# Experts' activations: 32 by 32 block transposes on VectorE in place of TensorE transposes, with the down weights' rows in the matching order

## The chip, the core and the metric

The kernel runs on one core of a Trainium2 chip. The metric is the device time of one execution in microseconds, lower is better. Before the change three timed runs gave 1387.32, 1388.30 and 1388.99 us, a median of 1388.3. All numbers are 32-bit floating point (some products use a split into a high and a low part).

## The reference

The model is a two-layer trunk on 256 tokens of width 1024. Layer 0 has an attention mixer and a dense feed-forward part, layer 1 a state-space mixer and a mixture of eight experts, of which each token takes its best two. The change lies in the experts:

```python
def moe_swiglu(h, w_router, w_gate, w_up, w_down):
    logits = (h @ w_router).astype(jnp.float32)
    top_val, top_idx = lax.top_k(logits, TOP_K)
    weights = jax.nn.softmax(top_val, axis=-1)
    gates = jnp.sum(jax.nn.one_hot(top_idx, N_EXPERTS, dtype=jnp.float32) * weights[..., None], axis=-2)
    out = jnp.zeros_like(h)
    for e in range(N_EXPERTS):
        out = out + gates[..., e:e + 1] * swiglu(h, w_gate[e], w_up[e], w_down[e])
    return out
```

Here `swiglu(h, g, u, d)` is `(silu(h @ g) * (h @ u)) @ d`. Gate and up weights are 1024 x 2816 for each expert, down weights 2816 x 1024.

## The kernel before

The experts are ranked by how many tokens chose them, and each rank has room for a fixed number of groups of 32 tokens: 4, 3, 3, 3, 3, 2, 2, 2 (`CAPS`). "Expert 0" below is the first rank. An expert's 2816 hidden columns are worked off in three blocks (`b`): 1024, 1024 and 768 (512 + 256).

For each block TensorE first does the gate and up products (`gate_up`, L1676). The tokens of group i are the stationary operand, 128 x 32, and the weights move. A weight unit is 128 rows by 1024 columns, 512 KB, one DMA. Its columns are cut in four pieces, each of which goes to its own 32 columns of the array, and so to its own 32 partitions of the result. So the PSUM bank `gu[i]` holds, at partition 32j + t, token t's columns of the j-th quarter. In the profile each such product is two records. ScalarE and VectorE then make silu(gate) * up of it (L1703 to L1708) in the tile `eh`, still with 32 tokens in each quarter of the partitions.

The down product (`down`, L1723) needs the hidden columns on the partitions, so `eh` is transposed between (`trans`, L1710): TensorE transposes 128 x 128 pieces into PSUM (L1715, L1717, and L1719 for the 64-row piece of the third block), and ScalarE or VectorE copy them to `hT` (L1721). `eh` and `hT` are two halves of one tile and both bear the name `eh` in the profile. There is one copy of each.

The order is written out in `experts` (L1742 to L1757): gate and up of block b, the down product of the block before, the transposes of block b, and so on. The transposes of block b thus stand between a down product and the next gate product, and their result is first read a whole gate and up product later. Only the very last down product (L1771) follows its transposes directly.

Other work, such as gathering the next expert's tokens (L1591), selecting them (L1580), multiplying the down result by its gate (L1627) and scattering it back (L1649), is put into a queue with a count of weight units and is issued between units (`run_queue`).

Weights come through one list of transfers on the SP queue in the order of use (L171). A transfer is issued when a buffer is free: 4 + 15 buffers, and two pairs (`hT_hi`, `hT_lo`) that earlier stages lend, 23 of 512 KB in all. A buffer is given back when TensorE has read it (`release`). After the experts stands a branch (`overflow`, L1788) for tokens that found no room; it was not taken in the profiled execution.

Of the kernel before, what the change touches and what calls it, by code (L numbers as in the profile page):

```python
# [12 lines left out]
AF = mybir.ActivationFunctionType  # L13
OP = mybir.AluOpType
AX = mybir.AxisListType

D = 1024
# [3 lines left out]
NE = 8  # L21
# [11 lines left out]
CAPS = (4, 3, 3, 3, 3, 2, 2, 2)  # L33
# [40 lines left out]
S_SW, S_W2, S_FB, S_B2, S_GN, N_SMALL = 0, 192, 448, 449, 451, 579  # L74


def layout(inputs):

    r = {n: np.ascontiguousarray(inputs[n]) for n in _INS}
    col = lambda v: v.reshape(-1, 128).T  # L80
    c = make_consts()
    c[:, C_C:C_C + 8] = col(inputs["c"])
    r["consts"] = c
    r["vecs"] = np.concatenate([inputs[m.replace("mod", "norm")].reshape(-1, 128) for m in NORMS]
                               + [inputs[m + "_b"].reshape(-1, 128) for m in NORMS])
    s = np.zeros((128, N_SMALL), np.float32)
    w = inputs["e_w_in"][0]
    s[:, S_SW:S_SW + 192] = np.concatenate([w[:, 1536:1544], w[:, 3080:3096]], axis=1).reshape(8, 128, 24) \
        .transpose(1, 0, 2).reshape(128, 192)
    s[40:56, S_W2:S_W2 + 256] = inputs["e_gla_w2"][0]  # L90
    for i in range(4):
        s[32 * i:32 * i + 8, S_FB] = inputs["e_fox_fb"].reshape(8)
    s[:, S_B2:S_B2 + 2] = col(inputs["e_gla_b2"])
    s[:, S_GN:S_GN + 128] = inputs["e_gla_norm"].reshape(1, 128)
    r["smalls"] = s

    st = lambda z: z.reshape(32, 2, 64).transpose(1, 2, 0).reshape(128, 32)
    dt = np.broadcast_to(inputs["o_log_dt"].reshape(32, 2, 1), (32, 2, 64))
    d = np.zeros((128, 32), np.float32)
    d[96:128] = inputs["o_d_skip"].reshape(32, 32).T  # L100
    r["s5par"] = np.concatenate([st(inputs["o_lam_re"]), st(inputs["o_lam_im"]), st(dt), d], axis=1)
    b = [inputs[n].reshape(32, 2, 64, 16).transpose(1, 2, 0, 3).reshape(128, 512) for n in ("o_b_re", "o_b_im")]
    c = [inputs[n].reshape(32, 2, 16, 64).transpose(1, 3, 0, 2).reshape(128, 512) for n in ("o_c_re", "o_c_im")]
    r["s5bc"] = np.concatenate(b + c, axis=1)


    z = np.stack([inputs["o_exp_gate"][0], inputs["o_exp_up"][0]], axis=2).reshape(NE, NCH, 128, 2, FF)
    z5 = z[..., 2 * D:2 * D + 512].reshape(NE, NCH, 128, D)
    z2 = z[..., 2 * D + 512:].reshape(NE, 4, 2, 128, 512).transpose(0, 1, 3, 2, 4).reshape(NE, 4, 128, D)
    r["o_exp_rest"] = np.concatenate([z5, z2], axis=1)  # L110
    return r


# [129 lines left out]
class Trunk:  # L243
# [1412 lines left out]
    def experts(self):  # L1656


        nc, ex, st, mm = self.nc, self.ex, self.st, self.nc.tensor.matmul
        do = lambda n, fn, *args: self.queue.append([n, lambda: fn(*args)])  # L1660
        hid = ex.tile([128, 2, 4, 256], F32, name="eh", tag="z", bufs=2)
        eh, hT = hid[:, 0], hid[:, 1]
        cg = lambda j: slice(32 * j, 32 * j + 32)
        bank = lambda n: self.psum.tile([128, 512], F32, name=n, tag=n, bufs=1)
        gu, dn = [bank(f"gu{i}") for i in range(4)], [bank(f"dn{i}") for i in range(2)]
# [10 lines left out]
        def gate_up(e, b):  # L1676
            xT = self.xT[e]
            def wide(o):
                def emit(i, k, raw):
                    for j in range(4):  # L1680
                        mm(gu[i][cg(j), o:o + 256], xT[:, k, cg(i)], raw[:, 256 * j:256 * j + 256],  # L1681
                           start=(o == 0 and k == 0), stop=(o > 0 and k == NCH - 1))
                return emit

            def rest(i, u, raw):
                for h in range(2):
                    for j in range(4):
                        w = raw[:, 512 * h + 128 * j:512 * h + 128 * j + 128]
                        if u < 8:
                            mm(gu[i][cg(j), 128 * h:128 * h + 128], xT[:, u, cg(i)], w, start=(u == h == 0),  # L1690
                               stop=False)
                        else:
                            mm(gu[i][cg(j), 256:384], xT[:, 2 * u - 16 + h, cg(i)], w, start=False,
                               stop=(u == 11 and h == 1))

            if b < 2:
                for n, o in (("o_exp_gate", 0), ("o_exp_up", 256)):
                    group(e, [(n, e, b, k) for k in range(NCH)], wide(o))
            else:
                group(e, [("rest", e, b, k) for k in range(12)], rest)  # L1700
            for i in range(CAPS[e]):
                w = 256 if b < 2 else 128
                nc.scalar.activation(eh[:, i, 0:w], gu[i][:, 0:w], AF.Silu)  # L1703
                nc.vector.tensor_tensor(out=eh[:, i, 0:w], in0=gu[i][:, w:2 * w], in1=eh[:, i, 0:w], op=OP.mult)  # L1704
                if b == 2:
                    o = eh[64:128, i, 128:256]
                    nc.scalar.activation(o, gu[i][0:64, 256:384], AF.Silu)
                    nc.vector.tensor_tensor(out=o, in0=gu[i][64:128, 256:384], in1=o, op=OP.mult)  # L1708

        def trans(e, b):  # L1710
            for x in range(0, CAPS[e], 2):
                n = min(2, CAPS[e] - x)
                p = self.ps([128, 2, 256])
                for i in range(n):
                    nc.tensor.transpose(p[:, i, 0:128], eh[:, x + i, 0:128], self.ident)  # L1715
                    if b < 2:
                        nc.tensor.transpose(p[:, i, 128:256], eh[:, x + i, 128:256], self.ident)  # L1717
                    else:
                        nc.tensor.transpose(p[:, i, 128:192], eh[64:128, x + i, 128:256], self.ident[64:128, 64:128])  # L1719
                w = 256 if b < 2 else 192  # L1720
                (nc.vector.tensor_copy if x else nc.scalar.copy)(hT[:, x:x + n, 0:w], p[:, :n, 0:w])  # L1721

        def down(e, b):  # L1723
            n = 8 if b < 2 else 6
            def emit(i, f, raw):
                c = (128 * (f % 2) + 32 * (f // 2)) if b < 2 else 32 * f
                for j in range(4):
                    mm(dn[i // 2][cg(j), 256 * (i % 2):256 * (i % 2) + 256], hT[:, i, c:c + 32],  # L1728
                       raw[:, 256 * j:256 * j + 256], start=(b == f == i % 2 == 0),
                       stop=(b == 2 and f == n - 1 and (i % 2 == 1 or i == CAPS[e] - 1)))  # L1730

            group(e, [("down", e, b, f) for f in range(n)], emit)
# [48 lines left out]
    def overflow(self):  # L1781

        nc, kp, ex, I = self.nc, self.keep, self.ex, self.ins
# [4 lines left out]
        with self.tc.If(self.most > 0):  # L1788
            for first in (0.0, 128.0):
                v.memset(cur, 1.0)  # L1790
                with self.tc.For_i(0, NE, 1) as e:
# [18 lines left out]
                    for k in range(NCH):  # L1810
                        p = self.ps()
# [4 lines left out]
                    p = self.ps()  # L1816
# [2 lines left out]
                        nc.tensor.transpose(p[:, 128 * t:128 * t + 128], P[:, t, :], self.ident)  # L1819
                    v.tensor_copy(B.rearrange("p t j -> p (t j)"), p[:, 0:256])  # L1820
                    dn = self.dn
                    raw = lambda n: self.rawpool.tile([128, D], F32, name=n, tag="raw", bufs=4)
                    w3 = lambda n, f: (I[n][0, bass.ds(e, 1), :, 128 * f:128 * f + 128]
                                       .rearrange("o (k p) f -> p (o k) f", p=128))
                    for f in range(FF // 128):
                        wg, wu, wd = raw("og"), raw("ou"), raw("od")
                        gv, uv = (z.rearrange("p (k f) -> p k f", k=NCH) for z in (wg, wu))
                        nc.sync.dma_start(out=gv, in_=w3("o_exp_gate", f))
                        nc.sync.dma_start(out=uv, in_=w3("o_exp_up", f))
                        nc.sync.dma_start(out=wd, in_=I["o_exp_down"][0, bass.ds(e, 1), 128 * f:128 * f + 128, :]  # L1830
                                          .rearrange("o p d -> p (o d)"))
                        b = self.ps()
                        for i, z in enumerate((gv, uv)):
                            for k in range(NCH):
                                nc.tensor.matmul(b[:, 128 * i:128 * i + 128], z[:, k, :], xT[:, k, :], start=(k == 0),
                                                 stop=(k == NCH - 1))
                        h = kp.tile([128, 2, 128], F32, name="oh2", tag="t2k", bufs=4)
                        a.activation(h[:, 0, :], b[:, 0:128], AF.Silu)
                        v.tensor_tensor(out=h[:, 1, :], in0=h[:, 0, :], in1=b[:, 128:256], op=OP.mult)
                        for x in range(2):  # L1840
                            nc.tensor.matmul(dn[x], h[:, 1, :], wd[:, 512 * x:512 * x + 512], start=(f == 0),
                                             stop=(f == FF // 128 - 1))
# [4 lines left out]
                    for t in range(2):  # L1847
                        for x in range(2):
                            hs = slice(512 * x, 512 * x + 512)
                            p = self.ps()  # L1850
# [346 lines left out]
```

## Time and profile before

| | |
|---|---|
| timed runs, median (range) | 1388.3 us (1387.32 to 1388.99) |
| profiled execution | 1385.76 us, of which the span of the program is 1384.0 us |
| TensorE products | 1254.3 us busy, 91% of the span |
| VectorE | 599.9 us, 43% |
| ScalarE | 380.6 us, 28% |
| bytes moved by DMA | 398.59 MB, mean 288 GB/s |
| mean granted TensorE clock | 0.956 of 2.4 GHz |

The experts' part runs from about 640 us to the end. A busy time says how long an engine had at least one instruction under way; the busy shares of the whole span mix this part with the earlier stages, in which VectorE has far more to do, so the parts are looked at one by one. Times in the rows below are counted from the span's start. "PE" is TensorE's product stream, "PEld" its loads of the stationary operand, DVE VectorE, ACT ScalarE, SPq the queue of the engine that issues the weights' transfers.

### The profile page before, as it was taken

The page shows a single profiled execution, that of the slowest core. Times are in us where ns is not written, and L with a number is a line of the kernel's source. Part 1 is how long each engine was busy: PE and PEld are TensorE (multiplying, and loading weights), DVE is VectorE, ACT ScalarE, POOL GpSimd, SP SyncE. Part 2 cuts the span into 40 slices and gives each one's busy share as a digit, 9 for nine tenths or more (in the row PEclk, how much of TensorE's full clock was granted, in tenths as well). Part 3 has the DMA queues.
Part 4 walks back from the last instruction along what each step waited for, and adds up shares of the span by engine and source line. Part 5 has one row for each costly group of instructions (what it writes and reads, how often), then busy time and mean ns, then how long its engine had stood idle before and what let it go on. Part 6 is the DMA issues. An engine that isn't in the chain of part 4 may idle for free. (4 is left out here: it accounts for less than half of the span.)

```text
span 1384.0 us, 42896 instructions
## 1 busy us (share of the span) xinstructions
PE 1254.3 (91%) x18767; PEld 956.9 (69%) x18767; DVE 599.9 (43%) x1023; ACT 380.6 (28%) x832; POOL 267.3 (19%) x324
## 2 busy tenths in 40 slices
PE   5998988789896878889989999999999999999985
PEld 4976777678795778775676676575586586756552
DVE  6998798678889685651000210210200202111113
ACT  4455444455543566520010110110010011101001
POOL 1000036999859252000000000000000000000000
PEclk9998999899998888999999999999999999999998
DMA  9866648678785211339998989989989989999994
GB/s 346 278 224 228 198 135 262 208 249 268 251 276 180 92 62 48 107 116 407 407 385 311 366 311 352 399 298 372 392 295 391 375 310 401 407 406 407 407 407 186
DMA packets 138723, 398.59 MB, mean 288 GB/s; under 512 B 12288, under 2 KB 45312, under 8 KB 138400
## 3 DMA queue, kind: packets, MB, share of 16 engines
q1 hardware_dynamic: 138176, 394.62, 78.7%
q8 instruction: 149, 2.44, 0.7%
q0 software_dynamic: 208, 1.15, 0.3%
q14 instruction: 46, 0.38, 0.1%
q10 hardware_dynamic: 144, 0.00, 0.0%
HBM read 394.67 MB, written 1.05 MB: 286 GB/s over the span
## 5 line engine op out<-in xcount | busy, mean ns | idle before, releaser
L1704 DVE TENSOR_TENSOR eh<-gu,eh 128x256 f32<-128x256 f32 (+1 forms) x66 | 25.1, 380 | 433.5 <-ACT eh L1703 432.9
L280 PE MATMUL ps<-hT_hi,hl 128*128 128x256 f32 x576 | 172.0, 299 | 16.1 <-ACT hT_hi L839 7.6
L205 DVE TENSOR_TENSOR hl<-raw,hl 128x1024 fp32r<-128x1024 f32 x121 | 158.5, 1316 | 61.1 <-ACT hl L198 59.3
L281 PE MATMUL ps<-hT_lo,hl 128*128 128x256 f32 x576 | 169.2, 294 | 3.0 <-DVE hT_lo L840 2.5
L282 PE MATMUL ps<-hT_hi,hl 128*128 128x256 f32 x576 | 168.8, 293 | 3.2 <-DVE hl L205 3.1
L1681 PE MATMUL gu<-raw,xTs 128*32 128x256 f32 x3032 | 168.7, 380 | 1.5 <-DMA raw<-in_o_exp_up_dram 1.5
L385 POOL TENSOR_TENSOR ss<-ss 128x1 f32<-128x1 f32 x10 | 2.7, 275 | 862.3 <-ACT ps L378 779.2
L198 ACT ACTIVATE hl<-raw 128x1024 fp32r<-128x1024 f32 x121 | 126.9, 1058 | 144.2 <-PE ps L282 32.3
L1681 PEld LDWEIGHTS gu<-raw,xTs 128*32 128x32 f32 x3032 | 97.3, 110 | 67.4 <-DMA raw<-in_o_exp_up_dram 3.9
L280 PEld LDWEIGHTS ps<-hT_hi,hl 128*128 128x128 f32 x576 | 115.7, 201 | 19.5 <-ACT hT_hi L839 8.1
L1728 PE MATMUL dn<-raw,eh 128*32 128x256 f32 x2032 | 119.1, 380 | 3.1 <-issue 2.0
L281 PEld LDWEIGHTS ps<-hT_lo,hl 128*128 128x128 f32 x576 | 115.6, 201 | 5.0 <-DVE hT_lo L840 3.4
L282 PEld LDWEIGHTS ps<-hT_hi,hl 128*128 128x128 f32 x576 | 115.3, 200 | 4.6 <-DVE hl L205 4.5
L1728 PEld LDWEIGHTS dn<-raw,eh 128*32 128x32 f32 x2032 | 69.7, 110 | 46.2 <-issue 6.6
L1703 ACT ACTIVATE eh<-gu 128x256 f32<-128x256 f32 (+1 forms) x66 | 23.0, 348 | 267.6 <-PE gu L1681 237.5
L1721 ACT COPY eh<-ps 128x512 f32<-128x512 f32 (+1 forms) x24 | 13.2, 550 | 231.7 <-PE ps L1717 155.0
L1681 PE MATMUL gu<-rawh,xTs 128*32 128x256 f32 x992 | 56.1, 380 | 0.6 <-DMA rawh<-in_o_exp_up_dram 0.6
L1721 DVE COPY eh<-ps 128x256 f32<-128x256 f32 (+3 forms) x15 | 6.8, 451 | 108.0 <-PE ps L1717 54.1
L1690 PE MATMUL gu<-raw,xTs 128*32 128x128 f32 x1664 | 51.5, 278 | 1.3 <-DMA raw<-in_o_exp_rest_dram 0.8
L1627 DVE TENSOR_TENSOR y<-dn,gate 32x256 f32<-32x256 f32 x88 | 36.9, 419 | 31.9 <-PE dn L1728 30.6
L1690 PEld LDWEIGHTS gu<-raw,xTs 128*32 128x32 f32 x1664 | 45.7, 112 | 4.7 <-DMA raw<-in_o_exp_rest_dram 2.3
L1681 PE MATMUL gu<-rawi,xTs 128*32 128x256 f32 x848 | 47.5, 379 | 0.0
(425 smaller groups left out, 2222.0 us busy)
## 6 DMA issues: line engine op xcount, KB each, us to landing
raw<-in_o_exp_down_dram SPq DMA_DIRECT2D x92, 512.0 KB, 8.9
raw<-in_o_exp_gate_dram SPq DMA_DIRECT2D x68, 512.0 KB, 6.2
raw<-in_o_exp_up_dram SPq DMA_DIRECT2D x67, 512.0 KB, 6.3
raw<-in_o_exp_rest_dram SPq DMA_DIRECT2D x58, 512.0 KB, 10.1
rawi<-in_o_exp_down_dram SPq DMA_DIRECT2D x30, 512.0 KB, 5.9
rawh<-in_o_exp_down_dram SPq DMA_DIRECT2D x27, 512.0 KB, 6.2
raw<-in_e_mod_ffn_w_dram SPq DMA_DIRECT2D x24, 512.0 KB, 4.4
raw<-in_o_mod_mix_w_dram SPq DMA_DIRECT2D x24, 512.0 KB, 4.6
```

Source lines behind the costliest of these rows:

```text
L198: nc.scalar.activation(hi, raw, AF.Copy)
L205: nc.vector.tensor_tensor(out=lo, in0=raw, in1=hi.bitcast(F32), op=OP.subtract)
L280: mm(out, lh, rh, start=start, stop=False)
L281: mm(out, lh, rl, start=False, stop=False)
L282: mm(out, ll, rh, start=False, stop=stop)
L1627: self.nc.vector.tensor_tensor(out=self.y[32 * i:32 * i + 32, cs], in0=self.dn[i // 2][js, o:o + 256], in1=self.gate[js, cs], op=OP.mult)
L1681: mm(gu[i][cg(j), o:o + 256], xT[:, k, cg(i)], raw[:, 256 * j:256 * j + 256], start=(o == 0 and k == 0), stop=(o > 0 and k == NCH - 1))
L1690: mm(gu[i][cg(j), 128 * h:128 * h + 128], xT[:, u, cg(i)], w, start=(u == h == 0), stop=False)
L1703: nc.scalar.activation(eh[:, i, 0:w], gu[i][:, 0:w], AF.Silu)
L1704: nc.vector.tensor_tensor(out=eh[:, i, 0:w], in0=gu[i][:, w:2 * w], in1=eh[:, i, 0:w], op=OP.mult)
L1721: (nc.vector.tensor_copy if x else nc.scalar.copy)(hT[:, x:x + n, 0:w], p[:, :n, 0:w])
L1728: mm(dn[i // 2][cg(j), 256 * (i % 2):256 * (i % 2) + 256], hT[:, i, c:c + 32], raw[:, 256 * j:256 * j + 256], start=(b == f == i % 2 == 0) ...
```

## The change

`trans` becomes one VectorE transpose for each group of tokens. It turns every 32 x 32 block of the tile in its place and moves no block to other partitions. With w columns in a quarter, the block at partitions 32j.. and columns 32f.. then holds hidden columns j*w + 32f + r on its rows r, so one slice of 32 columns of `hT` has, on its 128 partitions, four runs of 32 hidden columns that lie w apart. The host lays the rows of the down weights out in this order (`down_order`), so each transfer of 128 rows stays as it was. In the third block the last 256 columns are four quarters of 64 with gate and up side by side, so that its short operations are 128 x 64 and not 64 x 128. In the overflow branch one transfer becomes four.

```diff
+def down_order():
+    return np.concatenate([r0 + np.arange(4 * w).reshape(4, w // 32, 32).transpose(1, 0, 2).reshape(-1)
+                           for r0, w in ((0, 256), (D, 256), (2 * D, 128), (2 * D + 512, 64))])
...
-    z2 = z[..., 2 * D + 512:].reshape(NE, 4, 2, 128, 512).transpose(0, 1, 3, 2, 4).reshape(NE, 4, 128, D)
+    z2 = z[..., 2 * D + 512:].reshape(NE, 4, 2, 128, 2, 4, 64).transpose(0, 1, 3, 2, 5, 4, 6).reshape(NE, 4, 128, D)
...
+    r["o_exp_down"] = np.ascontiguousarray(r["o_exp_down"][:, :, down_order()])
...
-                    o = eh[64:128, i, 128:256]
-                    nc.scalar.activation(o, gu[i][0:64, 256:384], AF.Silu)
-                    nc.vector.tensor_tensor(out=o, in0=gu[i][64:128, 256:384], in1=o, op=OP.mult)
+                    o = eh[:, i, 128:192]
+                    nc.scalar.activation(o, gu[i][:, 256:320], AF.Silu)
+                    nc.vector.tensor_tensor(out=o, in0=gu[i][:, 320:384], in1=o, op=OP.mult)
...
         def trans(e, b):
-            for x in range(0, CAPS[e], 2):
-                n = min(2, CAPS[e] - x)
-                p = self.ps([128, 2, 256])
-                for i in range(n):
-                    nc.tensor.transpose(p[:, i, 0:128], eh[:, x + i, 0:128], self.ident)
-                    if b < 2:
-                        nc.tensor.transpose(p[:, i, 128:256], eh[:, x + i, 128:256], self.ident)
-                    else:
-                        nc.tensor.transpose(p[:, i, 128:192], eh[64:128, x + i, 128:256], self.ident[64:128, 64:128])
-                w = 256 if b < 2 else 192
-                (nc.vector.tensor_copy if x else nc.scalar.copy)(hT[:, x:x + n, 0:w], p[:, :n, 0:w])
+            w = 256 if b < 2 else 192
+            for i in range(CAPS[e]):
+                nc.vector.transpose(hT[:, i, 0:w], eh[:, i, 0:w])
...
-                c = (128 * (f % 2) + 32 * (f // 2)) if b < 2 else 32 * f
+                c = 32 * f
...
-                        nc.sync.dma_start(out=wd, in_=I["o_exp_down"][0, bass.ds(e, 1), 128 * f:128 * f + 128, :]
-                                          .rearrange("o p d -> p (o d)"))
+                        for i in range(4):
+                            r0 = rows.index(128 * f + 32 * i)
+                            nc.sync.dma_start(out=wd[32 * i:32 * i + 32], in_=I["o_exp_down"][0, bass.ds(e, 1),
+                                              r0:r0 + 32, :].rearrange("o p d -> p (o d)"))
```

TensorE's instructions of the kernel before, at the end of the down product that follows expert 4's first gate and up block (`dn` is the down result, `ps` the transposes' bank, `cst` holds the identity, `gu` the gate and up result):

```order
L1728 MATMUL dn_6284<-rawh,eh 32x256 x8
L1728 MATMUL dn_6285<-rawh,eh 32x256 x4
L1715 MATMUL ps_11556<-cst,eh 128x128
L1717 MATMUL ps_11556<-cst,eh 128x128
L1715 MATMUL ps_11556<-cst,eh 128x128
L1717 MATMUL ps_11556<-cst,eh 128x128
L1715 MATMUL ps_11562<-cst,eh 128x128
L1717 MATMUL ps_11562<-cst,eh 128x128
L1681 MATMUL gu_6280<-rawh,xTs 32x256 x4
L1681 MATMUL gu_6281<-rawh,xTs 32x256 x4
```

The same place on TensorE in the changed kernel, whose lines are numbered anew (the down product is L1729, the gate and up product L1689):

```order
L1729 MATMUL dn_6284<-rawh,eh 32x256 x8
L1729 MATMUL dn_6285<-rawh,eh 32x256 x4
L1689 MATMUL gu_6280<-rawh,xTs 32x256 x4
L1689 MATMUL gu_6281<-rawh,xTs 32x256 x4
L1689 MATMUL gu_6282<-rawh,xTs 32x256 x4
```

The six transposes are gone, and the gate product follows the down product directly.

VectorE's instructions of the kernel before, one section later in expert 4 (`X` is the result that the scatter is added to, `P` the next expert's selection):

```order
L1654 TENSOR_TENSOR X<-ps_11889,X 128x512
L1654 TENSOR_TENSOR X<-ps_11920,X 128x512
L1721 COPY eh<-ps_11943 128x256
L1580 TENSOR_SCALAR P<-cst,rpp 128x128 x2
L1704 TENSOR_TENSOR eh<-gu_6280,eh 128x128
L1708 TENSOR_TENSOR eh<-gu_6280,eh 64x128
```

The same place on VectorE in the changed kernel:

```order
L1662 TENSOR_TENSOR X<-ps_11795,X 128x512
L1662 TENSOR_TENSOR X<-ps_11826,X 128x512
L1722 STREAM_TRANSPOSE eh<-eh 128x256 x3
L1588 TENSOR_SCALAR P<-cst,rpp 128x128 x2
L1712 TENSOR_TENSOR eh<-gu_6280,eh 128x128
```

One copy out of PSUM has become three transposes from `eh` to `hT`, ahead of the selection for the next expert.

TensorE's instructions of the kernel before around the last transposes, those of expert 7's third block:

```order
L1728 MATMUL dn_6284<-hT_lo,eh 32x256 x16
L1715 MATMUL ps_14862<-cst,eh 128x128
L1719 MATMUL ps_14862<-cst,eh 128x64
L1715 MATMUL ps_14862<-cst,eh 128x128
L1719 MATMUL ps_14862<-cst,eh 128x64
L1728 MATMUL dn_6284<-raw_14432,eh 32x256 x8
```

The same place on TensorE in the changed kernel:

```order
L1729 MATMUL dn_6284<-hT_hi,eh 32x256 x16
L1729 MATMUL dn_6284<-hT_lo,eh 32x256 x16
L1729 MATMUL dn_6284<-raw_14296,eh 32x256 x8
L1729 MATMUL dn_6284<-raw_14306,eh 32x256 x8
L1729 MATMUL dn_6284<-raw_14316,eh 32x256 x8
```

Here the last down product stands directly behind the one before it, with VectorE's two transposes of 128 x 192 between them in time.

## Rows read from the trace of the kernel before

**Rows 1.** Windows: us, busy us of PE, PEld, DVE, ACT, POOL; clock; DMA share; GB/s.

```profile
700.00:720.00 20.00, 15.60 (x381) 14.75 (x377) 0.00 (x0) 1.67 (x6) 0.00 (x0) 0.83 1.02 406
...
860.00:880.00 20.00, 20.00 (x366) 12.01 (x360) 6.59 (x16) 2.46 (x5) 0.00 (x0) 1.00 1.03 405
...
1100.00:1120.00 20.00, 20.00 (x475) 16.55 (x478) 2.20 (x5) 3.16 (x9) 0.00 (x0) 1.00 0.81 284
...
1160.00:1180.00 20.00, 20.00 (x344) 11.35 (x340) 8.07 (x17) 2.80 (x5) 0.00 (x0) 1.00 1.03 407
```

**Rows 2.** Waits of the DMA queue, 640 to 1384 us: us in total, times, longest.

```profile
SPq L171 <- PE gu L1681: 112.1, 159, 2.4
```

**Rows 3.** Waits of PE, 640 to 1384 us.

```profile
PE gu L1693 <- issue: 8.2, 8, 1.7
...
PE gu L1681 <- DMA raw<-in_o_exp_up_dram: 1.5, 5, 0.7
```

**Rows 4.** Timeline of PE, expert 4, first block: start us, us, engine, line, operation.

```profile
1063.40 6.66 PE L1728 MATMUL dn<-rawh,eh 128*32 128x256 f32 x120
1069.99 0.33 PE L1715 MATMUL ps<-cst,eh 128*128 128x128 f32 x1
...
1070.59 0.27 PE L1717 MATMUL ps<-cst,eh 128*128 128x128 f32 x1
1070.79 1.50 PE L1681 MATMUL gu<-rawh,xTs 128*32 128x256 f32 x24
```

**Rows 5.** Timeline of PE around four other sections of transposes.

```profile
641.70 3.64 PE L1681 MATMUL gu<-hT_hi,xTs 128*32 128x256 f32 x64
...
646.67 3.66 PE L1681 MATMUL gu<-hT_lo,xTs 128*32 128x256 f32 x64
...
683.35 7.09 PE L1728 MATMUL dn<-raw,eh 128*32 128x256 f32 x128
...
691.39 5.45 PE L1690 MATMUL gu<-raw,xTs 128*32 128x128 f32 x192
...
730.17 9.01 PE L1728 MATMUL dn<-raw,eh 128*32 128x256 f32 x160
...
738.80 2.10 PE L1728 MATMUL dn<-rawh,eh 128*32 128x256 f32 x32
...
742.67 2.58 PE L1681 MATMUL gu<-rawh,xTs 128*32 128x256 f32 x44
...
1136.74 1.56 PE L1728 MATMUL dn<-rawa,eh 128*32 128x256 f32 x24
...
1139.62 5.60 PE L1681 MATMUL gu<-raw,xTs 128*32 128x256 f32 x100
```

**Rows 6.** Groups by line and shape on DVE, from 640 us: busy us, mean ns.

```profile
L1721 DVE COPY eh<-ps 128x256 f32<-128x256 f32 x8 | 3.4, 425 | 39.6 <-PE ps L1717 39.6
L1580 DVE TENSOR_SCALAR P<-cst,rpp 128x128 f32<-128x128 f32 x14 | 3.3, 278 | 0.0
...
L1543 DVE TENSOR_REDUCE rpl<-rcm 128x1 f32<-128x8 f32 x1 | 0.2, 161 | 0.0
```

**Rows 7.** Window from expert 4's last section on.

```profile
1138.00:1150.00 12.00, 12.00 (x203) 7.10 (x202) 0.36 (x1) 0.48 (x1) 0.00 (x0) 1.00 1.02 388
```

**Rows 8.** Timeline of PE around the last transposes.

```profile
1355.91 2.26 PE L1728 MATMUL dn<-hT_lo,eh 128*32 128x256 f32 x32 [0.29 <-DMA hT_lo<-in_o_exp_down_dram]
...
1359.72 4.78 PE L1728 MATMUL dn<-raw,eh 128*32 128x256 f32 x80 [0.62 <-ACT eh L1721]
...
1364.81 1.07 PE L1728 MATMUL dn<-rawh,eh 128*32 128x256 f32 x16 [0.31 <-DMA rawh<-in_o_exp_down_dram]
```

**Rows 9.** Waits of PE, expert 0's third block, 690 to 730 us.

```profile
PE gu L1693 <- issue: 3.0, 2, 1.6
PE ps L1591 <- issue: 2.8, 1, 2.8
```

**Rows 10.** Waits of PE, expert 4's third block, 1100 to 1130 us.

```profile
PE gu L1693 <- issue: 0.7, 1, 0.7
```

More of the change, by code (lines that the diff above doesn't have):

```diff
@@ L1821, in overflow @@
                     dn = self.dn
+                    rows = list(down_order())
                     raw = lambda n: self.rawpool.tile([128, D], F32, name=n, tag="raw", bufs=4)
```

## The prediction

> **What bounds the kernel now.** I read the windows first. In the eight experts' part (from about 640 us) TensorE is busy nearly all of every stretch at a granted clock of 1.00, while the transfers run at full pace, 407 GB/s, only in some: in experts 1 to 4 they fall to 284 GB/s in the stretch of the third block of columns, and from 1160 us on they stay at 407 [rows 1]. The waits say why. The DMA queue stood 112.1 us, in 159 places, behind TensorE's gate and up products alone, because a weight buffer comes free only when TensorE has read it [rows 2]; TensorE's longest wait of the other kind, for an up unit, is 1.5 us in all [rows 3]. So from 640 to about 1138 us TensorE sets the pace and the transfers wait for it; after that the experts have two groups of 32 tokens, TensorE needs 16 x 0.054 = 0.86 us for a 512 KB unit that takes 1.29 us to transfer (524288 bytes at 407 GB/s), and the transfers set the end, with some 23 buffers (4 + 15 + 4 in the code) of lead for TensorE to eat up. What TensorE saves before 1138 us therefore moves the end; what it saves after is lost in waits for data.
>
> **What is removed: TensorE's transposes.** A section of them stands behind each down block. Its cost is the start of the next product's first record, less the time at which that record would have come at the pace of the stream before. The pace is (738.80 - 730.17) / 160 = 0.054 us a record [rows 5]. Block 0 of expert 4 (three groups): 1063.40 + 120 x 0.054 = 1069.88, the next product starts at 1070.79, so six transposes cost 0.91 us [rows 4]. Expert 0 (four groups), in the same way: 646.67 - (641.70 + 64 x 0.054) = 1.51; 691.39 - (683.35 + 128 x 0.054) = 1.13; and with the 64-row transposes of the third block 742.67 - (738.80 + 32 x 0.054) = 2.14. The third block with three groups: 1139.62 - (1136.74 + 24 x 0.054) = 1.58 [rows 5].
>
> Up to 1138 us there are the three sections of expert 0 (4.78), eight of the 0.91 kind in experts 1 to 4 (7.28), and four of the 1.58 kind (6.32): 18.4 us. The last of these stands where the transfers are already nearly full: from 1138 to 1150 us they ran at 388 GB/s, so they had 12 x (1 - 388/407) = 0.56 us to give [rows 7]; I count that and not 1.58. The sum is 18.4 - 1.0 = 17.4 us. The eight sections of experts 5 to 7 that stand before the last one I price at nothing: the transfers there run at 407 GB/s, and a TensorE that is earlier waits longer for data.
>
> Does something else become late in a section's place? The next gate product overwrites the PSUM bank that ScalarE and VectorE read. Behind a down block they have been done for microseconds. Only the very first section has no down block ahead of it; there the four groups' products need their banks one by one, 8 x 0.054 = 0.43 us apart, and VectorE, whose operation on such a piece I take to cost what its copy does, 425 ns [rows 6], frees them at the same pace, so I let the 1.51 stand.
>
> **What is added: VectorE's transposes.** There are 66, 44 of 128 x 256 and 22 of 128 x 192. No row shows one. The nearest is the copy of the same 128 x 256 out of PSUM, 425 ns; less than the 278 ns of a 128 x 128 operation is not to be expected, and if each of the eight blocks of 32 columns cost a whole small operation (161 ns) it would be 1.29 us [rows 6]. I take 0.43, the copy that does the same work: 66 x 0.43 = 28 us at most, on a VectorE that is busy between 0 and 8.07 us of 20 in the four stretches shown [rows 1].
>
> Their cover: the result is wanted only after the next gate and up block, 12 or 16 units, that is 10 us or more. What queues behind them on VectorE, as they wait for the down block to end, is the selection for the next expert (two operations of 278 ns, wanted by TensorE's gather three units later, which is 3.9 us with three groups at 24 x 0.054 = 1.30 a unit) and, in another section, the down result's 32-row products, wanted 17 units later. Three transposes at 0.43 fit with room. At 1.29 the gather would come 3 x 1.29 + 0.56 - 3.9 = 0.5 us late, in five places before 1138 us: 2.6 us lost.
>
> The last section has no cover. The down block before it ends at 1355.91 + 2.26 = 1358.17, the final one starts at 1359.72 and needs its last weights at 1364.81 [rows 8]. Five units at 0.86 take 4.3 us, so it may start as late as 1360.5. Two transposes at 0.43 and a handover end about 1359.1: earlier than now, but the end still waits for the last transfer, so nothing is won. At 1.29 each it is 1360.8, 0.3 us lost.
>
> The rest costs nothing: 24 copies leave ScalarE and 15 VectorE, both with idle time. The third block's short part is computed in 128 x 64 instead of 64 x 128, behind a down block. The down weights' rows come in another order from the host, in transfers of the same shape. The four smaller DMAs are in the overflow branch, which this execution did not enter.
>
> **The sum.** The profiled execution took 1385.76 us, of which 1384.0 is the span; minus 17.4 it is 1368.4. It lies 2.5 us below the median of the three timed runs, 1388.3, on which the forecast stands: **1370.9 us**.
>
> **The rivals.** *A: part of the gain is already the transfers'.* In the wide stretches of experts 1 to 4 the transfers do run at 405 GB/s [rows 1]. If a section counts only where the queue is idle just then, the four wide sections of 0.91 and the four before a wide block (three of 1.58 and the 0.56) fall out: 17.4 - 3.6 - 5.3 = 8.5, giving 1379.8. Against it: in each expert there follows a stretch at about 290 GB/s, in which the lead is filled up again and the saved time is passed on.
>
> *B: slower, by stalls of TensorE's own.* In the third block it stops for no releaser that the profile shows: 8.2 us in eight places [rows 3]. In expert 0, where the transfers run at 406 GB/s and the mean clock is 0.83 [rows 1], it lost 3.0 + 2.8 = 5.8 us in this way, and in expert 4, at 284 GB/s, 0.7 [rows 9, 10, 1]. If a denser TensorE pulls the transfers up to full pace in the third blocks of experts 1 to 4, and the stalls come with it, each loses 5.1 more: 4 x 5.1 = 20.4, against 17.4 won, 1391.3. It decides from about 400 GB/s there. Against it: 3.4 us less (0.91 + 0.91 + 1.58) in an expert of 99 ((1139.62 - 742.67) / 4, [rows 5]) lifts 284 to about 294. The Trainium skill (Runtime: NRT & Kernel Launch, Instruction fetch mechanics) says that an engine's instructions come in blocks of 16 KiB over a DMA queue of its own, and that crossing a block's boundary is mostly hidden. By that rule a straight stream has no such stall and the time would be 1370.9; the rows disagree as far as 5.8 us in expert 0 go, though they name no cause.
>
> *C: the transfers are the bound throughout,* and nothing is won: 1388.3. Against it stand the 112.1 us of the DMA queue's waits.
>
> **How the numbers follow.** A difference under 0.2%, 2.8 us, can't be told from none. The forecast has 0.80, and its own range is 1368 (all of 18.4 and some of the stalls) to 1375 (VectorE at its upper price takes 2.6 + 0.3, and a stall or two lands elsewhere). A has 0.12, C 0.03, B 0.05. So faster 0.92, same 0.03, slower 0.05; the range that leaves out about a fifth is 1367 to 1377.
>
> **What would show it.** Right: no records on TensorE between the down block and the next gate products, the gate stream going on at 0.054 us; 128 x 256 transposes of about 0.43 us on VectorE; the start of steady 407 GB/s moved from about 1140 to about 1122 us; an end that follows the last weights as before. Wrong: TensorE waiting for data already in experts 1 to 4 (A), longer gaps without a releaser in the third blocks (B), transposes well over 1.3 us, or a last down block that starts after its last weights are there.

## The result, and the profile after

The changed kernel took 1372.3 us, the median of four runs (1370.2 to 1375.6), against 1387.8 for the kernel before beside it (1384.1 to 1389.0): a ratio of 0.9895 [0.9867, 0.9923], 15.5 us less. The forecast was 1370.9 in 1367 to 1377. The profiled execution took 1371.33 us, 14.4 less than the 1385.76 of before. Four runs of the experiments, of 1561 to 2833 us, fell into a second, slower state of the chip and are left out of every median and ratio below. I tell first how far the stages of the forecast show in the trace.

TensorE's timeline at the place of [rows 4], the first section of expert 4 (start us, us, engine, line, operation, out<-in):

```profile
1050.33 1.56 PE L1729 MATMUL dn<-raw,eh 128*32 128x256 f32 x24
1051.62 6.74 PE L1729 MATMUL dn<-rawh,eh 128*32 128x256 f32 x120
1058.10 1.56 PE L1689 MATMUL gu<-rawh,xTs 128*32 128x256 f32 x24
```

120 records at 0.054 us from 1051.62 end at 1058.10, and there the next gate product starts: the 0.91 us of the section are gone to the hundredth. VectorE's groups from 640 us on (busy us, mean ns of one, idle time before them and its releaser) give the price of what was put in their place:

```profile
L1722 DVE STREAM_TRANSPOSE eh<-eh 128x256 f32<-128x256 f32 x44 | 18.8, 441 | 54.5 <-PE dn L1729 54.5
L1722 DVE STREAM_TRANSPOSE eh<-eh 128x192 f32<-128x192 f32 x22 | 8.3, 378 | 42.1 <-PE dn L1729 41.3
```

27.1 us together, 441 ns where the copy of [rows 6] had 425. The same stretches as in [rows 1], and the one in which the full transfers now begin (us; busy us of PE, PEld, DVE, ACT, POOL; clock; DMA share; GB/s):

```profile
700.00:720.00 20.00, 14.51 (x432) 13.51 (x425) 0.00 (x0) 1.83 (x6) 0.00 (x0) 1.00 1.03 407
...
1100.00:1120.00 20.00, 19.65 (x525) 16.43 (x519) 1.44 (x6) 3.01 (x12) 0.00 (x0) 1.00 0.88 288
1120.00:1140.00 20.00, 20.00 (x376) 11.83 (x372) 1.99 (x5) 0.77 (x2) 0.00 (x0) 1.00 1.02 406
1140.00:1160.00 20.00, 20.00 (x378) 11.83 (x372) 7.42 (x17) 1.94 (x4) 0.00 (x0) 1.00 1.03 407
```

406 to 407 GB/s begin with 1120 where the forecast said 1122. Taken over expert 4's third block itself, the transfers ran at 281 GB/s before and 291 now; the forecast lifted 284 to 294:

```profile
1106.00:1127.70 21.70, 20.97 (x618) 19.95 (x621) 1.40 (x5) 4.25 (x14) 0.00 (x0) 1.00 0.83 281
...
1092.50:1113.80 21.30, 20.95 (x620) 19.94 (x616) 1.26 (x5) 3.30 (x11) 0.00 (x0) 1.00 0.87 291
```

The DMA queue now waits 96.7 us for the gate and up products of the first two blocks, 15.4 less than in [rows 2] (us in all, times, longest). That this is about the size of the gain is chance: its waits for all of TensorE's products are 263 us against 286.

```profile
SPq L179 <- PE gu L1689: 96.7, 151, 0.7
```

Where the gain goes can be followed by the start of the same product in both traces. The changed kernel's experts begin 0.6 us later (the stretch ahead is not changed), so 0.6 is to be added to what it is ahead. Some records of neighbouring products overlap, so the readings hold to 0.2 us:

```
same product, time in the trace of before         after is ahead by, us
end of expert 0's second gate section   691.4       2.1
first product of expert 1               742.7       3.2
                        2               845.0       7.7
                        3               943.5       9.9
                        4              1041.4      11.8
                        5              1139.6      15.5
inside expert 6                        1213.4      19.0
                                       1283.7      21.3
inside expert 7                        1303.4      16.8
                                       1322.4      13.9
last down product                      1365.5      14.3
```

TensorE gains until it has eaten its lead on the transfers, at 21.3 + 0.6 us, and gives 7.0 of it back in waits for weights. Its timeline shows that change-over, a unit each 1.28 us with 0.2 us of waiting, and then one long wait:

```profile
1281.36 1.07 PE L1729 MATMUL dn<-raw,eh 128*32 128x256 f32 x16 [0.21 <-DMA raw<-in_o_exp_down_dram]
1282.63 1.07 PE L1729 MATMUL dn<-raw,eh 128*32 128x256 f32 x16 [0.20 <-DMA raw<-in_o_exp_down_dram]
...
1308.51 1.07 PE L1729 MATMUL dn<-rawh,eh 128*32 128x256 f32 x16 [1.79 <-DMA rawh<-in_o_exp_down_dram]
```

The number that counts is therefore the lead at the time from which the transfers stay full, 15.5 + 0.6 = 16.1 us, and not the largest. The end, to be set beside [rows 8]:

```profile
1342.16 0.81 DVE L1722 STREAM_TRANSPOSE eh<-eh 128x192 f32<-128x192 f32 x2 [3.63 <-PE dn L1729]
1342.18 2.10 PE L1729 MATMUL dn<-hT_lo,eh 128*32 128x256 f32 x32
1344.18 0.62 PEld L1729 LDWEIGHTS dn<-raw,eh 128*32 128x32 f32 x16 [0.39 <-issue]
...
1346.71 2.27 PE L1729 MATMUL dn<-raw,eh 128*32 128x256 f32 x32 [0.25 <-DMA raw<-in_o_exp_down_dram]
...
1350.46 0.59 PEld L1729 LDWEIGHTS dn<-rawh,eh 128*32 128x32 f32 x16 [0.58 <-DMA rawh<-in_o_exp_down_dram]
```

The last two transposes run beside the down block before them, and the end waits for the last weights, as before.

What did not come as forecast is in the waits of TensorE from 640 us to 1124, where it still sets the pace (us in all, times, longest). These four rows are all; none names a transfer:

```profile
PE gu L1701 <- issue: 6.6, 6, 2.0
PE gu L1698 <- issue: 4.0, 3, 2.5
PE ps L1619 <- issue: 2.2, 1, 2.2
PE dn L1729 <- issue: 0.5, 1, 0.5
```

13.3 us without a releaser, which I call stalls. The same view of the kernel before, to 1138 us:

```profile
PE gu L1693 <- issue: 4.5, 5, 1.6
...
PE dn L1728 <- issue: 1.2, 2, 0.8
PE gu L1690 <- issue: 0.3, 1, 0.3
```

With the 2.8 us that stand in [rows 9] this is 8.8, so the changed kernel loses 4.5 us more in this way. The experiments ask three things: whether it is the sections up to expert 4 that were worth the time and VectorE really covers its share, what these stalls are, and what bounds the rest.

### The profile page after: what moved, and what is told of

It reads as the page before. It is cut to its first block, busy times and chain, and to the rows that moved or that the text cites. A ratio compares the mean times of both kernels' runs of the same rounds, so it can differ in the third digit from the quotient of the medians.

```text
span 1369.6 us, 42688 instructions
## 1 busy us (share of the span) xinstructions
PE 1234.4 (90%) x18635; PEld 991.2 (72%) x18635; DVE 622.3 (45%) x1074; ACT 364.7 (27%) x808; POOL 269.3 (20%) x324
## 5 line engine op out<-in xcount | busy, mean ns | idle before, releaser
L1689 PE MATMUL gu<-raw,xTs 128*32 128x256 f32 x3032 | 173.0, 379 | 2.7 <-DMA raw<-in_o_exp_up_dram 1.7
L1689 PEld LDWEIGHTS gu<-raw,xTs 128*32 128x32 f32 x3032 | 118.9, 110 | 51.4 <-DMA raw<-in_o_exp_up_dram 6.2
L288 PEld LDWEIGHTS ps<-hT_hi,hl 128*128 128x128 f32 x576 | 117.2, 204 | 16.7 <-DVE hT_hi L441 5.9
L1729 PE MATMUL dn<-raw,eh 128*32 128x256 f32 x2032 | 121.1, 380 | 3.1 <-DMA raw<-in_o_exp_down_dram 1.7
L290 PEld LDWEIGHTS ps<-hT_hi,hl 128*128 128x128 f32 x576 | 116.8, 203 | 6.2 <-DVE hl L213 6.2
L1729 PEld LDWEIGHTS dn<-raw,eh 128*32 128x32 f32 x2032 | 77.1, 110 | 40.2 <-DMA raw<-in_o_exp_down_dram 6.1
L1722 DVE STREAM_TRANSPOSE eh<-eh 128x256 f32<-128x256 f32 (+1 forms) x66 | 27.1, 420 | 96.5 <-PE dn L1729 95.8
L1613 ACT ACTIVATE xTs<-ps,colo_mod_ffn,colo_mod_ffn 128x96 f32<-128x96 f32 (+2 forms) x60 | 20.8, 422 | 164.9 <-PE ps L1599 163.9
L1689 PE MATMUL gu<-rawh,xTs 128*32 128x256 f32 x992 | 58.0, 379 | 0.6 <-DMA rawh<-in_o_exp_up_dram 0.6
L1698 PEld LDWEIGHTS gu<-raw,xTs 128*32 128x32 f32 x1664 | 45.3, 110 | 7.9 <-issue 5.6
L1689 PEld LDWEIGHTS gu<-rawh,xTs 128*32 128x32 f32 x992 | 37.3, 110 | 18.3 <-DMA rawh<-in_o_exp_up_dram 2.1
L1689 PE MATMUL gu<-rawi,xTs 128*32 128x256 f32 x848 | 49.4, 379 | 0.0
```

What stands on the lines that cost most here:

```text
L288: mm(out, lh, rh, start=start, stop=False)
L290: mm(out, ll, rh, start=False, stop=stop)
L1613: nc.scalar.activation(o, p[:, j, :], AF.Identity, bias=sh[:, k:k + 1], scale=A[:, k:k + 1])
L1722: nc.vector.transpose(hT[:, i, 0:w], eh[:, i, 0:w])
```

## The experiments

In the expectations T is the theory on record: only the sections before expert 5 count, and VectorE's work is covered. The other letters are its rivals, each told where it stands.

**Undo a half: the transposes put back for experts 0 to 4, or for 5 to 7.** VectorE's transposes stay; TensorE's are added in the old place, and nobody reads what they write.

```diff
+            if e < 5:          # t_early; t_late: if e >= 5
+                for x in range(0, CAPS[e], 2):
+                    p = self.ps([128, 2, 256])
+                    for i in range(min(2, CAPS[e] - x)):
+                        nc.tensor.transpose(p[:, i, 0:128], eh[:, x + i, 0:128], self.ident)
...
```

> The changed kernel, with TensorE's transposes put back for experts 0 to 4 as extra work: same number, same shapes, same place behind each down product, result read by nobody and copied by nobody. Theory T (the gain is TensorE's own time ahead of the point at about 1122 us from which the transfers run full): the 17.4 us come back, 1387 to 1391 us, equal to the kernel before within 3 us. Rival C (the gain is in what hung on the transposes: the 39 copies out of PSUM, the PSUM banks they held, waits for them): the copies are still gone, so 1372 to 1375 us.

> The same extra TensorE transposes, but for experts 5 to 7 alone, where the transfers run full. Theory T: TensorE has that time to spare there, 1371 to 1374 us, no more than 1.5 us above the changed kernel. Rival U (every section of transposes counts wherever it stands): eight sections of 0.7 to 1.3 us, 6.8 us together, 1379 us. Rival C as above: 1372 us too.

t_early took 1387.2 us, 0.9991 [0.9971, 1.0011] of before: the whole gain is gone. t_late took 1372.1, 0.9875 [0.9846, 0.9904]: nothing is gone. The unaltered changed kernel, timed beside them on the same chip (after_again, below), took 1376.0. The sections are there in both; t_early's timeline of TensorE shows expert 4's section of 0.91 us again, at 0.92:

```profile
1066.63 6.66 PE L1738 MATMUL dn<-rawh,eh 128*32 128x256 f32 x120
...
1074.03 1.50 PE L1689 MATMUL gu<-rawh,xTs 128*32 128x256 f32 x24
```

In t_late's one stands in expert 6 and costs 0.7 us of TensorE, but none of the time:

```profile
1241.67 1.07 PE L1738 MATMUL dn<-raw,eh 128*32 128x256 f32 x16
1242.67 0.33 PE L1727 MATMUL ps<-cst,eh 128*128 128x128 f32 x1
...
1243.26 2.83 PE L1698 MATMUL gu<-raw,xTs 128*32 128x128 f32 x96
```

This settles the step on which most of the sum rests: sections priced at 18.4 us before expert 5 give back 11 to 15 us of time (1387.2 against 1376.0 and 1372.3), and those behind it nothing. In the traces t_early lies 15.6 us behind the changed kernel at the first product of expert 5; its own stalls up to there are 8.6 us, not 13.3, and from 709 to 715 us it ran at a granted clock of 0.50. Rival C of these two runs, the copies out of PSUM and their banks, falls as well: the copies are gone from t_early, and its time is that of before.

**VectorE's work tripled.** Each of the 66 transposes is done three times.

```diff
-                nc.vector.transpose(hT[:, i, 0:w], eh[:, i, 0:w])
+                for _ in range(3):
+                    nc.vector.transpose(hT[:, i, 0:w], eh[:, i, 0:w])
```

> The changed kernel with each VectorE transpose done three times over (66 become 198, same input and output), so a group costs about 1.26 us where it cost 0.42. Theory T (VectorE is covered, but for the gather behind it at 0.5 us late in five places): 1372 to 1375 us. Rival V (VectorE's transposes stand on TensorE's path, as the wait that replaced the old one): 2 x 0.42 x 66 = 55 us at the most, 1427 us; a half of it would be 1400 us.

1371.8 us, 0.9892 [0.9859, 0.9925]: the same as the changed kernel, to within some 5 us. Its VectorE groups from 640 us:

```profile
L1723 DVE STREAM_TRANSPOSE eh<-eh 128x256 f32<-128x256 f32 x132 | 55.4, 436 | 57.5 <-PE dn L1730 54.5
L1723 DVE STREAM_TRANSPOSE eh<-eh 128x192 f32<-128x192 f32 x66 | 23.3, 370 | 43.8 <-PE dn L1730 42.3
```

51.6 us more of VectorE change nothing that is measurable, and rival V's 1400 to 1427 us is excluded; who waited for it is TensorE's loads in two places, 2.3 and 0.8 us. The prediction's upper price, 1.29 us a transpose, is about what three at 0.44 come to, so even that end would have stayed near the forecast.

**Fewer instructions for the same columns.** In the third block the host lays a gate piece of 128 columns beside its up piece, and one product of 256 columns takes the place of two of 128, in the eight units that hold both.

```diff
-    z5 = z[..., 2 * D:2 * D + 512].reshape(NE, NCH, 128, D)
+    z5 = z[..., 2 * D:2 * D + 512].reshape(NE, NCH, 128, 2, 4, 128).transpose(0, 1, 2, 4, 3, 5).reshape(NE, NCH, 128, D)
...
+                if u < 8:
+                    for j in range(4):
+                        mm(gu[i][cg(j), 0:256], xT[:, u, cg(i)], raw[:, 256 * j:256 * j + 256], start=(u == 0), stop=False)
+                    return
```

The reason lies in TensorE's weight loads of the changed kernel in expert 0's third block (the last field is the idle time before a group):

```profile
698.19 2.99 PEld L1698 LDWEIGHTS gu<-raw,xTs 128*32 128x32 f32 x110 [0.90 <-issue]
...
704.38 3.49 PEld L1698 LDWEIGHTS gu<-raw,xTs 128*32 128x32 f32 x128 [0.92 <-issue]
710.58 1.57 PEld L1698 LDWEIGHTS gu<-raw,xTs 128*32 128x32 f32 x59 [2.70 <-issue]
...
716.78 0.52 PEld L1621 LDWEIGHTS ps<-rgp,P 128*128 128x128 f32 x4 [2.37 <-issue]
...
722.97 1.78 PEld L1701 LDWEIGHTS gu<-hT_hi,xTs 128*32 128x32 f32 x66 [2.24 <-issue]
```

The stalls end 6.2 us apart, however long each of them is, and between the ends at 704.38 and 710.58 lie 128 loads, each with its product: 256 instructions. Counted through loads, products and the semaphore instructions between them, the stalls lie 256 records or a multiple of it apart, to within one record, in the traces of before, of after, of this run and of order_wide below. Meanwhile the weights come in at 407 GB/s (the first window above). The Trainium skill (Runtime: NRT & Kernel Launch, Instruction fetch mechanics) has instructions fetched in 16 KiB blocks of 256, by a DMA queue of their own, with the crossing mostly hidden. The distance agrees with the block, and the changed kernel's profile lists such a queue (packets, MB), with packets of 16,384 bytes each:

```profile
q8 instruction: 148, 2.42, 0.7%
```

The trace has the times of these packets. The five stalls above end 1.4 to 1.6 us after one of them has landed, and every stall over 0.25 us from 640 us on, in the traces of before, of after, of this run and of the order runs below, 1.2 to 1.6 us after one. So TensorE stands there until its next instructions have come. "Mostly hidden" agrees for the experts as a whole, where 17 of some 105 crossings show a stall in the changed kernel; in the third blocks beside full transfers it does not hold, with up to 2.7 us at a crossing.

> The changed kernel, with the third block's first eight units laid out by the host as gate and up side by side, so that one product of 256 columns takes the place of two of 128: as many columns, half the instructions in those units. In the traces so far TensorE's stalls without a releaser lie 256 instructions apart, or a multiple of it, and mostly in third blocks, where an instruction stands for the fewest columns. Theory S (TensorE outruns the supply of its own instructions there): expert 0's third block loses 1 to 3 us to such stalls where it lost 8.7, and the time falls to 1360 to 1368 us. Rival D (the stalls come with full transfers, whatever the instructions are): as many us lost there, 1370 to 1376 us.

1363.1 us, 0.9835 [0.9803, 0.9866]. Its TensorE has the same columns to do, 1231.0 us busy against 1234.4, in 17227 products against 18635. The instruction queue moves 11 packets less:

```profile
q8 instruction: 137, 2.24, 0.7%
```

11 blocks of 256 are 2816 instructions, the 1408 products that are saved and their 1408 loads. Waits of TensorE in expert 0's third block, 690 to 730 us, in the changed kernel and then in this run:

```profile
PE gu L1698 <- issue: 4.0, 3, 2.5
PE ps L1619 <- issue: 2.2, 1, 2.2
PE gu L1701 <- issue: 2.0, 1, 2.0
PE dn L1729 <- issue: 0.5, 1, 0.5
...
PE gu L1702 <- issue: 0.8, 1, 0.8
PE dn L1730 <- issue: 0.8, 1, 0.8
```

1.6 us where the changed kernel loses 8.7. From 640 us to the end the waits without a releaser fall from 19.2 to 3.3 us in the profiled execution, the fastest of this run; about 9 us of that reach the median, since TensorE's waits for weights begin sooner, at 1241 us and not at 1272.

**The experts' order.** Experts with two groups (5, 6, 7), where the transfers are the bound, are put between those with three, where TensorE is.

```diff
+ORD = (0, 5, 1, 2, 6, 3, 4, 7)
...
-        for e in range(NE):
+        for e, nx in zip(ORD, ORD[1:] + (None,)):
```

It is done on the changed kernel, on the kernel before, and on the changed kernel with the wide products.

> The changed kernel with the experts worked off in the order 0, 5, 1, 2, 6, 3, 4, 7 (groups of tokens 4, 2, 3, 3, 2, 3, 3, 2), the weights' list likewise. Theory T (TensorE sets the pace with three or four groups, the transfers with two, and the 23 buffers carry the one over the other): no stretch at the end in which TensorE waits for weights; of the 48 us in which the transfers stand idle today a good part is used, 1337 to 1347 us. Rival H (the transfers as a whole are the bound and the order of their use is indifferent): 1370 to 1376 us.

> The kernel before, transposes on TensorE, in the same order of experts. Theory T: TensorE is now the bound nearly to the end, so the transposes of all experts count, 18.4 us of experts 0 to 4 and 6.8 of the others; 22 to 27 us above the same order with VectorE's transposes, 1360 to 1371 us. Rival H: the same 15 us apart as in the old order.

> Both edits on the changed kernel: the new order of experts and the wide products in the third block. Theories T and S together: the gains add, as TensorE is the bound all through, 1325 to 1340 us, at least 5 us under the new order alone. Without S: no different from the new order alone, within 3 us.

order_after took 1362.6 us, 0.9831 [0.9799, 0.9863], and order_before 1383.8, 0.998 [0.9955, 1.0005]. Both miss what T and its rival forecast for them. Their difference, 21.2 us, lies just under the 22 to 27 of T and over the 15 of its rival: with the long stretch gone in which the transfers are the bound, the sections of experts 5 to 7 count as well. The traces bear it out: in neither does TensorE wait for a transfer after 640 us, and by the start of the same product order_after gains 2.6 us each in experts 5 and 6. The whole difference is not the sections' alone, though. order_after has 10.5 us more of stalls (26.5 against 16.0), and on the other side order_before ran at a granted clock of 0.51 to 0.58, where order_after has 1.00, from 710 to 717, 904 to 908 and 1174 to 1181 us. The size of order_after's own gain was missed by the stalls. Waits of TensorE in order_after from 640 us:

```profile
PE gu L1699 <- issue: 11.8, 9, 2.5
PE gu L1702 <- issue: 7.7, 6, 2.0
PE dn L1730 <- issue: 4.8, 5, 1.4
PE gu L1658 <- ACT yh L1644: 3.5, 1, 3.5
PE ps L1620 <- issue: 2.2, 1, 2.2
```

26.5 us without a releaser, and no wait for a transfer at all. The order lets more of the third blocks run beside full transfers, and there TensorE is busy for 15 to 16 of 20 us, as expert 0 was in the changed kernel:

```profile
880.00:900.00 20.00, 15.34 (x446) 13.77 (x439) 0.70 (x3) 3.09 (x11) 0.00 (x0) 1.00 1.03 407
1140.00:1160.00 20.00, 15.99 (x411) 14.40 (x399) 0.00 (x0) 3.23 (x10) 0.00 (x0) 1.00 1.02 406
```

So rival B's mechanism is real, but this change by itself did not move the third blocks of experts 1 to 4 to full transfers (279 to 291 GB/s in the changed kernel); another order does. order_wide, which takes away many of these instructions, took 1336.6 us (1335.3 to 1341.9), 0.9643 [0.9614, 0.9672]: 26 us under the order alone, and some 50 under the kernel before. It is the best version here. Its waits of that kind, in the same view:

```profile
PE dn L1731 <- issue: 3.1, 4, 1.0
PE gu L1703 <- issue: 2.9, 3, 1.0
```

**The wide products with and without the change.** With both kernels wide, most of the stalls are gone, and what the change is worth should show without them. The changed kernel with the wide products ran once more beside wide_before; after_again is the unaltered changed kernel, timed beside t_early, t_late and v_triple.

> The kernel before, transposes on TensorE, with the wide products in the third block, so that few instruction stalls are left on either side of the change. Theory S2 (of the 17.4 us of the sum the profile gave 14.4 because expert 0's third block lost 2.9 us more to stalls than before): without the stalls the change is worth its whole sum, so this kernel lies 16.5 to 19 us above the one below. Rival A (some sections were the transfers' own time and count for nothing): 8 to 14 us above it.

> The changed kernel with the wide products, once more, on the chip of the run above: 1360 to 1368 us by both theories.

> The changed kernel, unaltered, timed beside the three below on one chip, so that they have a level to be held against. Both theories: about 1372 us (four runs so far 1370.2 to 1375.6), 15 us under the kernel before.

wide_before took 1377.9 us, 0.994 [0.992, 0.9959], wide_again 1364.4, 0.9853 [0.9828, 0.9877]: 13.5 us between the medians, under the forecast of 16.5 to 19 and within the 8 to 14 of rival A. The experts' part in the profiles, from the first gate product to the end of the last down product, took 738.6 and 722.8 us, 15.8 apart, and 720.9 in the earlier run of the same wide kernel, which would be 17.7. Two stalls of 2.2 us in the loads (1.7 in the products) that wide_before's trace lacks stand in wide_again's. In the times, differences of 2 us between runs hide what I wanted to see: inconclusive. The traces show it at the place that counts. At the first product of expert 5, with the starts of the experts made equal, wide is 18.7 us ahead of wide_before and wide_again 16.9. Up to there wide has 3.3 us of stalls, wide_before 3.9 and wide_again 5.1. With the differences in stalls taken off, the lead is 18.1 both times, where the prediction had summed 18.4 up to that place; rival A's 8 to 14 does not fit that. after_again had a median of 1376.0, 0.9907 [0.9873, 0.9941], so the gain of the change itself is known to within about 4 us: the two ratios agree in their intervals, and both medians lie in the range.

## Why the prediction was right, step by step

- *TensorE bounds to about 1138 us, the transfers from there.* Right, and shown by taking the two halves back: 1387.2 and 1372.1 us. The prediction's C, nothing won, falls with the result. A (1379.8) falls with the waits and with the lead: no wait of TensorE names a transfer before 1124, and at expert 5 the lead was 16.1 us where A left 8.5, with the wide stretches at 405 GB/s all the same.
- *Sections of 1.51, 1.13, 2.14, 0.91 and 1.58 us, 18.4 us.* The sections went with the prices read from [rows 4, 5]: at the second gate section 2.1 + 0.6 = 2.7 us were won, where 1.51 + 1.13 = 2.64 had been worked out. Up to expert 5 the lead was 16.1, 2.3 short of 18.4. The term that was mis-sized is the stalls, which the sum held constant: 13.3 us against 8.8. That is 4.5 more, but 2.4 of them lie between the products of expert 0's third block and cost almost nothing there. The window at clock 0.83 [rows 1] holds a stretch, 705 to 711 us, at a granted clock of 0.50 (1.2 GHz), which began in a stall of 2.8 us; the changed kernel has 1.00 there, although it too stalls for 2.5. The block takes the same time in both (before, then after), and what the clock took and what the stalls took cancel to 0.2 us:

```profile
691.40:726.80 35.40, 29.49 (x806) 28.11 (x809) 1.41 (x5) 4.12 (x14) 0.00 (x0) 0.90 1.00 384
...
689.30:724.90 35.60, 27.40 (x812) 25.66 (x808) 1.50 (x6) 3.90 (x13) 0.00 (x0) 1.00 1.01 398
```

This 0.2 and the other 2.1 us of stalls are the 2.3 that were missing, as closely as the lead can be read.

- *The last section counts only 0.56, so 17.4.* The lead of 16.1 at 1139.6 and the final gain, 14.4 + 0.6 = 15.0 by the profile, are 1.1 apart, where the sum took off 1.0. The size agrees; that it is the same microsecond is argued, not shown.
- *VectorE at 0.43 us, covered.* Measured 0.44 and 0.38. The cover is wider than was claimed: three times the work costs nothing that is measurable.
- *The last section: earlier, and the end waits for the weights.* Right. I had let the two transposes wait for the down block's end at 1358; they ran beside its last two units. VectorE can write them so early because the last columns of that tile, which those units still read, are not written by the 192-wide transpose.
- *Rival B.* The condition, about 400 GB/s in the third blocks of experts 1 to 4, did not come about, at 291 GB/s in expert 4. The stalls grew all the same where the transfers were full already: in expert 0 from 5.8 us [rows 9] to 8.7. B's price was about right for the case in which they spread: the two third blocks with three groups that run at 407 GB/s in order_after lose 5.7 and 5.8 us, where B had 0.7 + 5.1, and the whole of order_after 26.5.

## What to carry to other kernels

Price a saved microsecond by the stretch in which it lies: it counts up to the place from which the transfers stay full, and the lead that an engine gains after it is given back. A stall without a releaser on TensorE is not noise to be held constant: count the instructions between two of them, and where the distance is 256, make the same columns with fewer instructions before anything else. Two changes that gain little alone (order 10 us, wide products 9) can gain 36 together, when one takes away what bounds the other.

## What the runs showed that was not expected

- The stalls at every 256th instruction of TensorE cost up to 2.7 us each beside transfers of 407 GB/s in the stretch of short products, and 0 to 2.2 us at about 290 GB/s. They are waits for TensorE's own instructions: each ends just after a packet of the instruction queue has landed, and fewer instructions remove them. Where stalls follow each other, their ends, and so the blocks, come 6.2 us apart at 407 GB/s, 5.7 at 303 (after, 915.99 to 921.65 us) and 5.1 at 286 (before, 824.58 to 834.81). That the weight transfers slow the fetch fits this; no run took the transfers away alone, so it is not shown.
- order_wide has 6.0 us of them with transfers of 396 GB/s and more all the way to 1300 us, and they cost at most 1.0 us each. With one block of instructions in 6.2 us, 128 products of 128 columns are used up too soon, in 3.7 us (704.38 to 708.08), and 128 of 256 columns at 0.054 us are not, in 6.9. That this longer distance hides the crossings is a reading that fits, not one that was tried by itself.
